# Two per-head factors spread over rows by transfers through DRAM instead of by products, with new figures for transfers in the planner

## The chip, the cores and the metric

The kernel runs on one core of one Trainium2 chip. Its engines are TensorE (PE, with its weight loads shown apart as PEld), VectorE (DVE), ScalarE (ACT), GpSimd (POOL) and SyncE (SP), which issues all transfers here. The metric is device microseconds of one execution; the time given is the median of three runs.

## What is computed

One step of a hybrid trunk layer: 2048 prompt tokens and 8 sample sequences of 16 tokens, width 1024. After an RMS norm one projection feeds three head groups: forgetting attention (6 heads), RWKV-7 time mixing (6 heads of 64) and cross-attention to 256 memory tokens (4 heads). Each group is gated, and an output projection with the residual ends the layer. The change touches the RWKV group. Cut to it, the reference is:

```
kk = k * ph(k_k)
kk = kk * lax.rsqrt(jnp.maximum(jnp.sum(kk * kk, axis=-1, keepdims=True), 1e-24))
...
S, y = rwkv_scan(s0, r, decay, k, v, kk, a)     # S <- S diag(w) + S (-kk)^T (a*kk) + v^T k
mu = jnp.mean(y, axis=-1, keepdims=True)
var = jnp.mean(jnp.square(y - mu), axis=-1, keepdims=True)
yn = (y - mu) * lax.rsqrt(var + GN_EPS) * ph(gn_w) + ph(gn_b)
```

Both the key's norm and the group norm's variance are one number for each token and head, with which all 64 rows of that head are multiplied.

## The kernel before, in words

The RWKV group holds its data with a pair of heads on the 128 partitions (64 rows a head) and tokens along the free dimension. The first phase of the program runs over four blocks of 512 tokens, and in each over three head pairs p; the 128 sample tokens come as three more groups, one behind each of three prompt groups. So there are 15 groups: 12 of 512 tokens (nt = 4 tiles of 128) and 3 of 128 (nt = 1). For a block, the normalised input xk is projected with weights that are split in two parts (tiles w, read back from the DRAM copy w_d from the second block on): pjd for the columns that stay transposed, pjt for q, k, v of the attention. A group passes through rwkv_in, rwkv_mid, rwkv_scan and rwkv_out, and projections of other columns lie between them.

per_head (line 342) sums the squares of a head's 64 rows by products with a matrix of ones (PSUM tile pss) and copies the result, a 128 x 2nt tile with tokens on partitions, to inv. In rwkv_in it is the key's norm: DVE takes the maximum and the reciprocal (lines 379 and 380), and since kk enters the update twice, that reciprocal is applied once: it is spread and multiplied into AR's first half (line 400), which the Gram products gr read with bk. In rwkv_out it is the variance: DVE and POOL make the inverse root (rsqrt_small, line 68 for DVE, 62 for POOL), and the spread factor is multiplied into ysb, half of tile yd (line 649).

spread (line 353) turns such a tile into 128 rows x 128nt tokens: for each token tile and head one product of the column, broadcast to 64 columns, with the identity. That is 8 calls of mm for 512 tokens and 2 for 128, into the single PSUM buffer "ra" that pss, zw, za and pbn use as well. The tile yd shares its buffer "bt" with rwkv_mid's tile bt. In the profile nearly every matmul has line 59 (mm), and DVE and POOL operations have 62, 65 and 68 (tt, stt, ts): they are told apart by their tiles.

The second phase is the attention, the sample sequences' attention and the output projection; it reuses the first phase's memory. There too a factor is spread over rows through DRAM (rc to rd, then two transfers rb<-rd, lines 1190 and 1193).

The order on every engine is not that of the code. _arrange collects all instructions, gives each a cost (_Op), and _schedule places them one by one, each where its engine could start it earliest, in a simulated run; it tries several rankings, keeps the shortest and writes that order out. An SP transfer has an issue time (own), a time on the wire (wire, one after another for all transfers) and a time to land (time). SP's queue works in order: an instruction there that waits holds up all behind it. A change of any cost can move instructions anywhere in the program.

Of the kernel before, what the change touches and what calls it, by code (L numbers as in the profile page):

```python
# [9 lines left out]
F32 = mybir.dt.float32  # L10
# [41 lines left out]
def kernel(ctx: ExitStack, tc: tile.TileContext, I: dict, O: dict):  # L52
    nc = tc.nc
    V, S, G, PE, SY = nc.vector, nc.scalar, nc.gpsimd, nc.tensor, nc.sync
# [3 lines left out]
    def mm(out, lhsT, rhs, start=True, stop=True):  # L58
        PE.matmul(out, lhsT, rhs, start=start, stop=stop, skip_group_check=True)  # L59

    def tt(e, out, a, b, op):
        e.tensor_tensor(out=out, in0=a, in1=b, op=op)  # L62

    def stt(out, a, s, b, op0, op1):
        V.scalar_tensor_tensor(out=out, in0=a, scalar=s, in1=b, op0=op0, op1=op1)
# [9 lines left out]
    M, A_, SUB, MAX = ALU.mult, ALU.add, ALU.subtract, ALU.max  # L75
# [21 lines left out]
    ident = ct("ident", [128, 128])  # L97
# [25 lines left out]
    with ExitStack() as p1:  # L123
# [12 lines left out]
        vh = c1t("vh", [128, 24])  # L136
# [25 lines left out]
        sm = pools(p1, "sm", bufs=2)  # L162
# [175 lines left out]
        def at(h, a=0):  # L338

            return slice(64 * (h ^ a), 64 * (h ^ a) + 64)  # L340

        def per_head(sq, nt):

            pss = ps.tile([128, 512], F32, tag="ra", name="pss")
            for t in range(nt):
                for j in range(2):
                    mm(pss[64 * j:64 * j + 64, 2 * t:2 * t + 2], sq[:, 128 * t + 64 * j:128 * t + 64 * j + 64],
                       bones[:, 0:128:64].bitcast(F32))
            r = sm.tile([128, 8], F32, tag="inv", name="inv")[:, :2 * nt]
            V.tensor_copy(r, pss[:, :2 * nt])  # L350
            return r

        def spread(r, nt, pool, tag):

            out = pool.tile([128, 512], F32, tag=tag, name="spr")
            for t in range(nt):
                for h in range(2):
                    mm(out[at(h), 128 * t:128 * t + 128], r[:, 2 * t + h:2 * t + h + 1].to_broadcast([128, 64]), ident)
            return out[:, :128 * nt]

        def rwkv_in(p, k, r, v, g, sample, tok0):

# [34 lines left out]
            V.tensor_copy(wc, wx[:, :, seg])  # L397

            stt(seg3(ar[:, 0, :n]), seg3(k), col(NKK), wx[:, :, 0:seg], M, M)
            tt(V, ar[:, 0, :n], ar[:, 0, :n], spread(inv, nt, ps, "ra"), M)  # L400
            tt(V, seg3(ar[:, 1, :n]), seg3(r), wx[:, :, 1:seg + 1], M)

            ts(G, e5, e3, col(HKA), col(OHKA), M, A_)
# [233 lines left out]
        def rwkv_out(p, sample, n, nch, tok0, gt, bv, py, so):  # L637

            nt = n // 128
            two = rv.tile([128, 2, 512], F32, tag="bt", name="yd")  # L640
            ysb, sq = two[:, 0, :n], two[:, 1, :n]
            S.copy(ysb, py.rearrange("p c t -> p (c t)")[:, :n])
            yc = pg.tile([128, 512], F32, tag="gr", bufs=2, name="yc")[:, :n]
            mm(yc, centre, ysb)
            S.activation(sq, yc, AF.Square)
            S.copy(ysb, yc)
            r = per_head(sq, nt)
            rsqrt_small(r, r, 2 * nt, 1.0 / 64, GN_EPS)
            stt(ysb, ysb, vh[:, GW5 + p:GW5 + p + 1], spread(r, nt, ps, "ra"), M, M)
            stt(bv, bv, vh[:, GB5 + p:GB5 + p + 1], ysb, A_, A_)  # L650
            tt(V, bv, bv, gt, M)
            SY.dma_start(o_d[384 + 128 * p:384 + 128 * (p + 1), tok0:tok0 + n], bv)
            if sample:
                for c in range(2):
                    pt = pg.tile([128, 512], F32, tag="gr", bufs=2, name="pst")
                    for s in range(4):
                        PE.transpose(pt[0:64, 128 * s:128 * s + 128], so[:, c, s, :], ident)
                    sst = rv.tile([64, 4, 2, 64], F32, tag="gm", name="sst", bufs=2)
                    S.copy(sst, pt[0:64, :].rearrange("p (s h k) -> p s h k", h=2, k=64))
                    for h in range(2):  # L660
                        SY.dma_start(O["rs_s"][4 * c:4 * c + 4, 2 * p + h].rearrange("s v k -> v s k"), sst[:, :, h, :])
# [882 lines left out]
class _Op:  # L1544


    def __init__(self, i, eng):
        ins, outs = ([s.bass_ap for s in x if getattr(s, "bass_ap", None) is not None] for x in (i.ins, i.outs))
        aps, kind = ins + outs, type(i).__name__
        space = lambda a: str(getattr(a.tensor, "_space", ""))  # L1550
        sizes = [_free(list(a.ap)) for a in ins]
        n = max(_free(list(a.ap)) for a in aps)
        self.shares = self.reads = self.two = False
        if eng == "PE":
            x, w = ins[:2]
            wide = str(i.ins[0].dtype) == "dt.float32"
            rows, cols, self.n = list(x.ap)[0][1], sizes[1], sizes[0]
            self.turns, self.plain, self.bf = i.is_transpose, wide and not i.is_transpose, "bf" in str(i.ins[0].dtype)
            size = lambda k: 32 if k <= 32 else 64 if k <= 64 else 128
            self.shape = (size(rows), size(cols)) if self.plain else (128, 128)  # L1560
            self.place = tuple(i.tile_position or (0, 0))
            self.load = 2 * cols / 2.4
            self.cells = self.n * rows / 128 * ((2 if self.turns else 4) if wide else 1)
            if self.plain:
                self.own = 2 * max(cols, self.n) / 1.2 + (10 if rows > 64 else 2)
                self.time = self.own + 165
            else:
                self.own = 30 if self.turns else 40 if self.bf else max(3 + 0.4453 * self.n, 12 + 0.4219 * self.n)
                self.time = 275 if self.turns else self.n / 2.4 + 170
            return  # L1570
        psum = any("PSUM" in space(a) for a in aps)
        scalar = n > 1 and any(k == 1 for k in sizes)
        if eng == "SP":
            size = 4 * list(outs[0].ap)[0][1] * _free(list(outs[0].ap))
            run = min(4 * list(a.ap)[-1][1] if list(a.ap)[-1][0] == 1 else 4 for a in aps)
            self.own, self.wire = (430 if run < 512 else 360), size / 230
            self.time = 1300 + (size / 140 - size / 230) * (run < 1024) / 2
            return
        wide = sum(k > 1 and "SB" in space(a) for k, a in zip(sizes, ins))
        self.reads = wide > 0  # L1580
        if eng == "Activation":
            t = (140 if psum else 178) + 0.833 * n + 90 * scalar
        elif eng == "Pool":
            if "pow" in str(getattr(i, "op", "")):
                t = 360 + 163 * n
            elif "Memset" in kind:
                t = 95 + 0.83 * n
            elif "ScalarPtr" in kind:
                t = 210 + 1.09 * n if n > 256 else 190 + 2.1 * n
            else:  # L1590
                t = 200 + 2.13 * n
        else:
            self.two = not psum and sum(k > 1 for k in sizes) == 1 and ("TensorCopy" in kind or "TensorScalar" in kind)
            self.shares = self.two or wide > 1
            if "Memset" in kind:
                t = max(65, 57 + 1.04 * n)
            elif "Reciprocal" in kind:
                t = 148 + 6.3 * n
            elif "Custom" in kind:
                t = 220 + 1.042 * n  # L1600
            else:
                t = 155 + 0.521 * n if self.two else 152 + 1.042 * n + 52 * (scalar and "ScalarPtr" in kind)
        self.time, self.own = t, t - _BACK[eng]
# [178 lines left out]
def _schedule(p, rank, stay, loose=()):  # L1782
# [33 lines left out]
    while len(order) < count:  # L1816
# [37 lines left out]
        c = cost[nodes[x][0]]  # L1854
        if e == "SP":
            free[e] = s + c.own
            wire = max(wire, s + c.own + 300) + c.wire
            end[x] = wire + c.time
        elif e == "PE":
            for j, k in enumerate(nodes[x]):  # L1860
                t, till = array.run(cost[k], r)
                s, end[x] = (t if not j else s), max(end[x], till)
            free[e] = array.last
        else:
            wait = 0
            if e == "DVE" and c.shares:
                wait = max([b - s for a, b, z in held["Pool"][-4:] if a < s < b and (c.two or z.reads)], default=0)
            elif e == "Pool":
                wait = max([b - s for a, b, z in held["DVE"][-4:] if a < s < b and (z.two or c.reads)], default=0)
            free[e], end[x] = s + wait + c.own, s + wait + c.time  # L1870
            if e == "Pool" or c.shares and e == "DVE":
                held[e].append((s + wait, free[e], c))
# [156 lines left out]
```

## Time and profile before

| | |
|---|---|
| runs (median, lowest, highest) | 1825.83, 1825.49, 1829.49 us |
| profiled execution: time / span | 1826.43 / 1824.6 us |
| mean granted TensorE clock | 0.967 |
| DMA queue's share of 16 engines | 48.5% |
| HBM read / written | 202.58 / 87.08 MB |
| first phase ends, attention begins | about 1131 us |

The page's busy shares are averages over the whole span, so the stages have to be looked at one by one. In rows of groups, "out<-in" names the tiles (buffer numbers left out), then come partitions x elements, the count, busy us, mean ns of one and the idle time of the engine just before them. In timelines the first two columns are start and length in us, and brackets give the idle time before a row and what ended it. "SPq" rows are issues of transfers by SP; their length is SP's issue time, not the time until the data lands.

### The profile page before, as it was taken

How to read it: one execution, taken by the hardware profiler on the slowest of the kernel's cores; microseconds unless marked ns; L12 is line 12 of the kernel's file. 1: busy time of each engine (PE TensorE's matmuls, PEld its weight loads, DVE VectorE, ACT ScalarE, POOL GpSimd, SP SyncE). 2: the span in 40 equal slices, each digit the busy share in tenths (PEclk: the TensorE clock that was granted, in tenths of full speed). 3: DMA queues.
4: the chain of work that ended last, by engine and by line, in shares of the span. 5: the costliest groups of instructions: out<-in, count | busy, mean ns of one | idle time of the engine just before them, and what ended most of it. 6: DMA issues, size and time to landing. Idle time of an engine off the chain costs nothing.

```text
span 1824.6 us, 41978 instructions
## 1 busy us (share of the span) xinstructions
PE 1756.1 (96%) x16883; PEld 1395.2 (76%) x16883; DVE 927.2 (51%) x2102; ACT 895.5 (49%) x1755; POOL 793.7 (43%) x818
## 2 busy tenths in 40 slices
PE   7999999999999999998999998999999999999998
PEld 6998999788877888876788886666666566667776
DVE  5544444464445553545743453767455545575213
ACT  5424343524234323324332434887888477986452
POOL 4555342242131341311332152567676265876452
PEclk8999999999999999999999999899999589999999
DMA  6767463745446464535363353434437542354422
GB/s 193 242 206 242 138 203 113 240 164 174 139 153 203 148 220 163 161 102 178 108 220 131 124 156 120 155 117 156 152 124 242 181 160 87 124 174 145 159 99 97
DMA packets 208905, 292.42 MB, mean 160 GB/s; under 512 B 56844, under 2 KB 161790, under 8 KB 192838
## 3 DMA queue, kind: packets, MB, share of 16 engines
q1 hardware_dynamic: 208710, 289.73, 48.5%
q8 instruction: 133, 2.18, 0.5%
q14 instruction: 62, 0.51, 0.1%
HBM read 202.58 MB, written 87.08 MB: 159 GB/s over the span
## 4 chain that ended last, share of the span: by engine, by line
PE 79%; DVE 7%; ACT 5%; DMA 3%; issue 3%; SPq 1%; POOL 1%; DVEq 0%; ACTq 0%; POOLq 0%
PE pjd L59 20%; PE pjt L59 12%; PE py L59 10%; PE po L59 9%; PE pS L59 7%; PE pm L59 4%; PE sc L59 2%; PE sy L59 1%; PE gr L59 1%; PE pz L59 1%; PE pa L59 1%; PE spr L59 1%; DMA w<-w_d 1%; PE gw L59 1%; PE gx L59 1%
## 5 line engine op out<-in xcount | busy, mean ns | idle before, releaser
L59 PE MATMUL pjd<-xk,w 128*128 128x512 f32 (+4 forms) x2280 | 522.6, 373 | 8.9 <-DVE xk L62 4.1
L59 PEld LDWEIGHTS pjd<-xk,w 128*128 128x128 f32 (+1 forms) x2280 | 380.4, 190 | 75.6 <-issue 10.2
L62 POOL TENSOR_TENSOR Pl<-P,Ph 128x512 fp32r<-128x512 f32 (+3 forms) x272 | 315.4, 1170 | 158.5 <-ACT Ph L1137 122.2
L59 PE MATMUL pjt<-w,xk 128*128 128x256 f32 x2040 | 282.4, 290 | 6.8 <-issue 3.5
L59 PEld LDWEIGHTS pjt<-w,xk 128*128 128x128 f32 x2040 | 260.1, 193 | 16.0 <-issue 7.8
L59 PE MATMUL py<-W,oh 128*128 128x512 f32 x816 | 248.7, 404 | 1.4 <-DVE rb L1179 1.4
L1134 ACT ACTIVATE P<-pS,NB 128x512 f32<-128x512 f32 x240 | 148.7, 623 | 70.8 <-PE pS L59 48.6
L59 PEld LDWEIGHTS py<-W,oh 128*128 128x128 f32 x816 | 150.1, 189 | 40.3 <-DVE rb L1179 1.8
L1078 DVE TENSOR_REDUCE mx<-pm 128x1 f32<-128x512 f32 (+2 forms) x240 | 140.8, 605 | 63.5 <-PE pm L59 60.7
L59 PE MATMUL pS<-Q,K 128*128 128x512 f32 (+1 forms) x480 | 162.6, 397 | 7.8 <-ACT P L1134 3.2
L1137 ACT CAST Ph<-P 128x512 fp32r<-128x512 f32 (+3 forms) x272 | 151.8, 564 | 18.6 <-PE po L59 13.7
L59 PE MATMUL po<-Ph,vt 128*65 128x512 f32 x480 | 156.8, 380 | 0.9 <-ACT ob L1157 0.5
L62 DVE TENSOR_TENSOR xo<-py,xo 128x512 f32<-128x512 f32 x68 | 46.7, 687 | 154.6 <-PE py L59 154.6
L59 PEld LDWEIGHTS pS<-Q,K 128*128 128x128 f32 (+1 forms) x480 | 88.7, 197 | 40.2 <-ACT P L1134 14.0
L62 POOL TENSOR_TENSOR nr<-nr,mhalf 128x8 f32<-128x8 f32 (+2 forms) x43 | 60.9, 1416 | 115.5 <-DVE nr L68 102.0
L59 PE MATMUL pm<-K,Q 67*128 67x512 f32 (+2 forms) x240 | 97.8, 424 | 2.8 <-DVE mx L1078 2.1
L62 POOL TENSOR_TENSOR w<-wraw,w 128x1024 fp32r<-128x1024 f32 (+1 forms) x34 | 79.8, 2348 | 43.8 <-ACT w L197 43.4
L59 PE MATMUL po<-Pl,vt 128*65 128x512 f32 x240 | 90.5, 377 | 0.2
L59 PEld LDWEIGHTS po<-Ph,vt 128*65 128x65 f32 x480 | 64.5, 142 | 26.5 <-issue 3.0
L710 ACT COPY qk<-pjt 128x512 f32<-128x512 f32 (+1 forms) x47 | 26.2, 565 | 102.5 <-PE pjt L59 63.3
L62 POOL TENSOR_TENSOR oh<-ot,oh 128x384 fp32r<-128x384 f32 (+2 forms) x38 | 45.9, 1207 | 61.6 <-ACT oh L1340 51.0
L59 PEld LDWEIGHTS pm<-K,Q 67*128 67x128 f32 x240 | 49.4, 209 | 20.3 <-DVE mx L1078 8.3
(399 smaller groups left out, 2847.4 us busy)
## 6 DMA issues: line engine op xcount, KB each, us to landing
w<-w_d SPq DMA_DIRECT2D x84, 1024.0 KB
w_d<-w SPq DMA_DIRECT2D x28, 1024.0 KB
y_d<-xo SPq DMA_DIRECT2D x21, 512.0 KB
wraw<-in_w_in SPq DMA_DIRECT2D x36, 256.0 KB
xo<-in_x SPq DMA_DIRECT2D x17, 512.0 KB
xo<-y_d SPq DMA_DIRECT2D x17, 512.0 KB
xt<-in_x SPq DMA_DIRECT2D x24, 256.0 KB
xraw<-in_xT SPq DMA_DIRECT2D x24, 256.0 KB
```

The lines of the kernel that those rows point to most:

```text
L59: PE.matmul(out, lhsT, rhs, start=start, stop=stop, skip_group_check=True)
L62: e.tensor_tensor(out=out, in0=a, in1=b, op=op)
L710: S.copy(o_, out)
L1078: V.tensor_reduce(out=q["mx"][:, h, t, c0 // 512:c0 // 512 + 1], in_=pm[:, :n], op=MAX, axis=AX.X)
L1134: S.activation(P_[:, c0:], pS[:, c0:], AF.Exp, bias=NB[:, qb, 2 * hp + h, kt:kt + 1] if fox else 0.0)
L1137: S.copy(Ph[:, c0:], P_[:, c0:])
```

## The change

spread no longer multiplies. It transposes the 128 x 2nt tile r to 2nt rows of 128 tokens (PE, PSUM tile spt), copies that to SBUF (ACT, tile spr), writes it to DRAM (SP, sp_d, 4 KB), and reads it back for each head with one transfer that gives the same 128nt numbers to 64 partitions (128 KB each). per_head now places its columns head by head, so that a head's rows lie together in sp_d. The target is given by the caller: AR's second half, which holds the squares before and the receptance after, and sq, the other half of yd. The products that follow read SBUF in place of PSUM. Besides, the planner's figures for transfers change.

```
                 for j in range(2):
-                    mm(pss[64 * j:64 * j + 64, 2 * t:2 * t + 2], sq[:, 128 * t + 64 * j:128 * t + 64 * j + 64],
+                    mm(pss[64 * j:64 * j + 64, t:t + nt + 1:nt], sq[:, 128 * t + 64 * j:128 * t + 64 * j + 64],
                        bones[:, 0:128:64].bitcast(F32))
...
-        def spread(r, nt, pool, tag):
-
-            out = pool.tile([128, 512], F32, tag=tag, name="spr")
-            for t in range(nt):
-                for h in range(2):
-                    mm(out[at(h), 128 * t:128 * t + 128], r[:, 2 * t + h:2 * t + h + 1].to_broadcast([128, 64]), ident)
-            return out[:, :128 * nt]
+        def spread(out, r, nt):
+
+            n = 2 * nt
+            pt = ps.tile([128, 512], F32, tag="ra", name="spt")
+            PE.transpose(pt[0:n, 0:128], r, ident)
+            rr = sm.tile([8, 128], F32, tag="spr", name="spr", bufs=1)[:n]
+            S.copy(rr, pt[0:n, 0:128])
+            sp_d = dt("sp_d", [8, 128], bufs=4)
+            SY.dma_start(sp_d[:n], rr)
+            for h in range(2):
+                SY.dma_start(out[at(h)], sp_d[nt * h:nt * h + nt].rearrange("t p -> (t p)").partition_broadcast(64))
...
-            tt(V, ar[:, 0, :n], ar[:, 0, :n], spread(inv, nt, ps, "ra"), M)
+            spread(ar[:, 1, :n], inv, nt)
+            tt(V, ar[:, 0, :n], ar[:, 0, :n], ar[:, 1, :n], M)
...
-            stt(ysb, ysb, vh[:, GW5 + p:GW5 + p + 1], spread(r, nt, ps, "ra"), M, M)
+            spread(sq, r, nt)
+            stt(ysb, ysb, vh[:, GW5 + p:GW5 + p + 1], sq, M, M)
...
-            self.own, self.wire = (430 if run < 512 else 360), size / 230
-            self.time = 1300 + (size / 140 - size / 230) * (run < 1024) / 2
+            self.own, self.wire = (430 if run < 512 else 360), size / (270 if run < 1024 else 340)
+            self.time = 700
...
-            wire = max(wire, s + c.own + 300) + c.wire
+            wire = max(wire, s + c.own + 600) + c.wire
```

PE around the first inverse norm, before (AR_0_117 is AR's first buffer; zw and za are products of the decay and the learning rate):

```order
L59 MATMUL pss<-bones,AR_0_117 64x2 x8
L59 MATMUL pjd<-xk,w 128x256 x3
L59 MATMUL zw<-LW,WUP 128x512
L59 MATMUL pjd<-xk,w 128x256 x12
L59 MATMUL za<-LW,WUP 128x512
L59 MATMUL pjd<-xk,w 128x256 x9
L59 MATMUL pjd<-xk,w 128x384 x2
L59 MATMUL spr<-ident,inv 64x128 x8
L59 MATMUL pjd<-xk,w 128x384 x22
L59 MATMUL pjt<-w,xk 128x256 x15
L59 MATMUL gr_795<-AR_0_117,bk 64x128
```

The same place on PE after the change:

```order
L59 MATMUL pss<-bones,AR_0_117 64x2 x8
L59 MATMUL pjd<-xk,w 128x256 x12
L59 MATMUL pjd<-xk,w 128x384
L59 MATMUL pjd<-xk,w 128x256
L59 MATMUL pjd<-xk,w 128x384 x6
L59 MATMUL zw<-LW,WUP 128x512
...
L357 MATMUL spt<-ident,inv 8x128
L59 MATMUL pjd<-xk,w 128x256 x23
L59 MATMUL pjd<-xk,w 128x384 x24
L59 MATMUL pjt<-w,xk 128x256 x58
L59 MATMUL gr_794<-AR_0_117,bk 64x128
```

Between the spread and the first Gram product stood 37 projection matmuls, and there stand 105 now.

SP at the same place, after the change (wraw and w_d are weights read and their split copy written):

```order
L196 DMA wraw<-in_w_in 128x4x128 x2
L200 DMA w_d<-w 128x2048
L361 DMA sp_d<-spr 8x128
L363 DMA AR_0_117<-sp_d 64x512 x2
L196 DMA wraw<-in_w_in 128x4x256
L200 DMA w_d<-w 128x2048
```

The broadcasts follow straight on the write that they wait for, and weights come behind them. So it is in 14 of the 30 spreads; in the other 16 one to nine other transfers stand between.

PE at the end of the first phase, before (the last group norm; pst turns the RWKV state for the output, pt and pS are the attention's first products):

```order
L59 MATMUL pss<-bones,yd 64x2 x8
L59 MATMUL pjd<-xk,w 128x512 x9
L59 MATMUL spr<-ident,inv 64x128 x8
L927 MATMUL pst<-ident,ST 64x128 x3
L998 MATMUL pt<-ident,tok 128x128 x8
```

And after the change:

```order
L59 MATMUL pss<-bones,yd 64x2 x8
L59 MATMUL sc<-st,AD 128x64
L59 MATMUL pjd<-xk,w 128x512 x9
L357 MATMUL spt<-ident,inv 8x128
L59 MATMUL pjd<-xk,w 128x512 x9
L754 MATMUL ptok<-ident,tsb 128x128 x4
L933 MATMUL pst<-ident,ST 64x128 x3
L1004 MATMUL pt<-ident,tok 128x128 x8
```

Nine projection matmuls and four transposes stand now between the last spread's step on PE and the attention's first products, where only pst stood.

## The prediction

> **What bounds the kernel now.** I read first the page's busy times and its chain, then busy time by stage, then the added and removed tiles, and last single moments in the timelines. The page says which engine is full and which work the end hangs on:
>
> ```profile
> PE 1756.1 (96%) x16883; PEld 1395.2 (76%) x16883; DVE 927.2 (51%) x2102; ACT 895.5 (49%) x1755; POOL 793.7 (43%) x818
> PE 79%; DVE 7%; ACT 5%; DMA 3%; issue 3%; SPq 1%; POOL 1%; DVEq 0%; ACTq 0%; POOLq 0%
> ```
>
> TensorE is busy for 1756.1 of 1824.6 us and carries 79% of the chain that ends last; DMA carries 3%. The other engines are at half. By stage (columns: stage, length, busy time of PE, PEld, DVE, ACT and POOL with instruction counts, granted clock, DMA share, GB/s), where the first two rows are the projections and the RWKV groups, and the rest is attention and output:
>
> ```profile
> 0.00:50.00 50.00, 39.62 (x181) 34.61 (x182) 29.85 (x69) 29.03 (x65) 23.05 (x34) 0.90 0.70 210
> 50.00:1135.00 1085.00, 1051.62 (x13148) 901.06 (x13147) 538.04 (x1388) 388.69 (x812) 357.13 (x391) 0.99 0.51 167
> 1135.00:1400.00 265.00, 258.62 (x1216) 176.09 (x1214) 157.70 (x271) 217.13 (x396) 175.37 (x165) 0.96 0.47 150
> 1400.00:1475.00 75.00, 69.50 (x384) 44.39 (x382) 43.62 (x100) 39.16 (x77) 27.14 (x32) 0.66 0.60 199
> 1475.00:1825.00 350.00, 336.70 (x1964) 239.03 (x1962) 157.97 (x279) 221.44 (x408) 210.98 (x198) 0.98 0.38 131
> ```
>
> Both spreads lie in the stage 50 to 1135 us: PE is idle there for only 33.4 of 1085 us, at a granted clock of 0.99. So there a microsecond of TensorE work is nearly a microsecond of time, as long as other matmuls can move into its place. The DMA engines are half free (0.51).
>
> **What is removed.** The spread's products, from the matmul groups with shapes kept apart (busy us, mean ns, idle before), and one of them in PE's timeline, between two projections:
>
> ```profile
> L59 PE MATMUL spr<-ident,inv 128*64 128x128 f32 x408 | 28.9, 280 | 0.0
> ...
> 214.13 0.28 PE L59 MATMUL pjt<-w,xk 128*128 128x256 f32 x1
> 214.34 1.09 PE L59 MATMUL spr<-ident,inv 128*64 128x128 f32 x16
> 215.36 0.44 PE L59 MATMUL pjd<-xk,w 128*128 128x384 f32 x1
> ```
>
> 408 records are 204 calls of mm (two passes each): 12 full spreads of 8 calls at each of two places, and 3 sample spreads of 2 calls at each. A full one holds PE from 214.34 to 215.36, 1.02 us; 24 of them are 24.5, and the group with the six small ones is 28.9. No idle stands before it, so PE reached each with its operand ready. Removed: **-28.9 us** of a full engine.
>
> **What PE does instead.** One transpose per spread, of a 128x8 tile against the identity. The nearest row is the transpose of a 128x9 tile; for a lower bound, four wide transposes back to back:
>
> ```profile
> L853 PE MATMUL psh<-ident,sho 128*9 128x128 f32 x13 | 3.3, 272 | 0.0
> ...
> 1131.35 0.63 PE L998 MATMUL pt<-ident,tok 128*128 128x128 f32 x4
> ```
>
> 3.3 / 13 = 0.25 us each; back to back it is (0.63 - 0.27) / 3 = 0.12, with 0.27 as the length of a lone one (272 ns). The new ones stand alone between matmuls of other shapes, so I take the first: 30 x 0.25 = **+7.6 us**, with 3.6 and 8.2 (30 x 0.272) as ends. The Trainium skill (TensorEngine Tiling, Key Properties) says that a change of tiling mode drains the engine; by it the transpose, a narrow tile among full ones, would cost its lone 0.27 and the sum would stand 0.6 us higher. The 128x9 rows, at 0.25, nearly agree.
>
> **What goes to other engines, and what hides it.** ACT gets 30 copies like the first row below (237 ns), 7 us on an engine that is busy for 388.7 of 1085 us. DVE's two products read SBUF in place of PSUM. Their times now (min/median/max ns) are the second and third row; with all operands in SBUF the like is the fourth:
>
> ```profile
> L855 ACT COPY shr<-psh 9x128 f32<-9x128 f32 x1 | 0.2, 237 | 0.0
> ...
> L62 DVE TENSOR_TENSOR AR<-AR,spr x15: 273/674/687, 74.9 to 1020.4; 128x512 f32<-128x512 f32 x12, 128x128 f32<-128x128 f32 x3
> L65 DVE SCALAR_TENSOR_TENSOR yd<-yd,vh,spr x15: 348/746/748, 215.5 to 1130.2; 128x512 f32<-128x512 f32 x12, 128x128 f32<-128x128 f32 x3
> ...
> L62 DVE TENSOR_TENSOR ob<-ob,rb x19: 680/694/1668, 1185.4 to 1722.0; 128x512 f32<-128x512 f32 x19
> ```
>
> The median stays, and now and then one may take 1 us more; DVE is half idle in that stage, so all this is 0. The 90 new transfers carry 24 x 260 KB and little else: at 167 GB/s in a stage with DMA half idle, no bound.
>
> What costs is latency. A spread now is a 4 KB write, whose landing SP awaits, and two broadcasts of 128 KB. Near rows: 64 KB and 8 KB landing, from the chain; and the same pair of broadcasts of the attention stage, from SP's first issue to the release of DVE, behind a 512 KB store:
>
> ```profile
> 303.83 1.94 DMA ld<-yt
> ...
> 309.04 1.65 DMA xd<-ld
> ...
> 1717.69 1.25 SPq L1193 DMA_DIRECT2D rb<-rd  x2
> 1721.99 0.69 DVE L62 TENSOR_TENSOR ob<-ob,rb 128x512 f32<-128x512 f32 x1 [4.72 <-DMA rb<-rd]
> ```
>
> 1.65 + (1721.99 - 1717.69) = 5.95 us, and with transpose and copy (0.5) a round trip of 6.5 us in place of 1.1. The Trainium skill (DMA: Bandwidth & Descriptors, Anatomy of one DMA) gives a transfer a fixed cost of about 2.0 us, mostly the wait for the write's receipt, and its Rules for kernel authors count transfers under 64 KB as mostly overhead; both speak against the change. By 2.0 for the write the round trip would be 6.9 us, and the tail below and the sum 0.4 us later. The 8 KB row, 1.65, is less.
>
> Cover for it: the inverse norm (DVE's reciprocal) is ready long before the Gram products gr that use it, or shortly before. The rows come in pairs, ready and used; the first and third pair are the first head pair of a token block, the second is the usual case, the fourth the group norm's product and the next writer of its buffer:
>
> ```profile
> 68.86 0.20 DVE L380 RECIPROCAL inv<-inv 128x8 f32<-128x8 f32 x1
> 77.25 0.43 PE L59 MATMUL gr<-AR,bk 64*64 64x128 f32 x2
> ...
> 141.20 0.19 DVE L380 RECIPROCAL inv<-inv 128x8 f32<-128x8 f32 x1
> 194.31 1.10 PE L59 MATMUL gr<-AR,bk 64*64 64x128 f32 x32
> ...
> 359.73 0.20 DVE L380 RECIPROCAL inv<-inv 128x8 f32<-128x8 f32 x1
> 369.43 1.10 PE L59 MATMUL gr<-AR,bk 64*64 64x128 f32 x32
> ...
> 351.86 0.75 DVE L65 SCALAR_TENSOR_TENSOR yd<-yd,vh,spr 128x512 f32<-128x512 f32 x1 [4.42 <-PE spr L59]
> 353.49 0.42 ACT L548 COPY bt<-pbt 128x128 f32<-128x128 f32 x2
> ```
>
> Usually there are 53 us (141.20 to 194.31). The first head pair of a block has 8.4 to 9.7 us, against a round trip plus product of 7.2: covered, and in the new order 105 projection matmuls stand between the first transpose and gr, where 37 did. The group norm's factor holds the yd buffer some 5 us longer; only a sample group's bt (353.49, right behind the last reader of yd) follows closely, and PE has projections meanwhile. So 0 here, with the rival below for where it fails.
>
> **The end of the stage** has no such cover. The last group norm's chain ends in DVE's product, and POOL fills the attention's K right behind it:
>
> ```profile
> 1129.28 4.71 DMA vtok<-v_d
> ...
> 1130.20 0.74 DVE L65 SCALAR_TENSOR_TENSOR yd<-yd,vh,spr 128x512 f32<-128x512 f32 x1
> 1130.96 0.99 POOL L990 MEMSET K<- 1x512 f32 x2
> ```
>
> If K waits for yd's memory, it comes 5 us later; but vtok lands only at 1134.0 (1129.28 + 4.71), so 3 of the 5 are covered: **+2 us**, ends 0 and 5.
>
> **The planner's new figures** change the whole order, in attention too. For 8 KB they go from 2.08 us (430 + 300 + 36 + 1300 + 11 ns) to 1.76, where the row has 1.65; for 64 KB from 2.25 to 1.85 (row 1.94); for a 1 MB weight load from 6.5 to 4.74, where the trace has
>
> ```profile
> 392.96 5.98 DMA w<-w_d
> ```
>
> So they are nearer for small transfers, and 1.2 us too hopeful for big ones, where the old were 0.5 too cautious. Too hopeful a load makes PE wait; too cautious a one only has other work put first. I take 0, and as ends a third of the 33.4 us of idle either way, an estimate: -11 to +11.
>
> **Sum**, against the profiled execution's 1826.43 us (span 1824.6 and 1.8 around it; the median of the three timed runs, 1825.83, is the same within 0.03%): -28.9 + 7.6 + 2 + 0 = -19.3, so **1807.1 us**. The ends of transposes, tail and planner give 1826.4 - 28.9 + 3.6 + 0 - 11 = 1790 and 1826.4 - 28.9 + 8.2 + 5 + 11 = 1822.
>
> **Rivals.** *SP holds the spreads up (slower).* SP is one queue in order, and it stands for matmuls in front of weight loads (total us, times, longest):
>
> ```profile
> SPq L192 <- PE pjd L59: 104.7, 45, 7.9
> ...
> 825.00:850.00 25.00, 19.96 (x398) 14.38 (x396) 9.22 (x14) 9.78 (x20) 5.19 (x6) 0.86 0.67 235
> ```
>
> A write or a broadcast behind such a load is late by up to 7.9 us, and in 14 of the 30 spreads the broadcasts follow straight on the write, so that SP itself stands for its landing, with weights queued behind. The tight places are four (first head pairs) and three (sample groups). A hold of 7.9 less the spare 1.2 to 2.5 us (8.4 or 9.7 less 7.2) leaves PE some 6 us idle, and the clock drops with it (0.86 where PE was busy for 19.96 of 25 us). It decides from a mean of 2.8 us at the seven places (19.3 / 7); 6 us at four of them, 24 us, give 1807 + 24 = 1831. Against it: the planner knows of SP's order, and PE is idle for little now despite those waits. *A longer cold stretch (no change).* The stage 1400 to 1475 had a clock of 0.66, so some 51 us (0.34 / 0.5 of 75) at half clock, worth up to 25 us. It is planned anew: 36 us more of it cost 18, which gives 1825. *A shorter one (faster still)*: half of it gone is -12, which gives 1795. *That the change does less than it says*: not so, the new order has no spr product and 30 transposes.
>
> **Chances.** Forecast (1800 to 1818) 0.58; part of the gain eaten, but still faster, 0.04; faster still 0.14; no change 0.12; slower 0.12. A difference of 0.2%, 3.7 us, is about what a measurement of this kernel can tell from none. Faster 0.58 + 0.04 + 0.14 = 0.76, same 0.12, slower 0.12. The range runs from 1793 (most of the faster case) to 1826 (all the forecast's ends and half of no change), leaving out some 0.2.
>
> **What would show it.** Right: PE's busy time falls by about 21 us, all of it before the attention, whose start moves from 1135 to about 1117; PE's idle stays near 70 us; gr waits for bk and not for AR's broadcast; the psh-like transposes take 0.25. Wrong: PE waits on transfers sp_d or on AR; SP's waits for the sp_d landing grow past 60 us with PE's waits on weights; the clock by stage differs from 0.99 before or 0.66 in the sample stage; or the attention stage, untouched by the spread, changes its length by more than 5 us.

## The result, and the profile after

| | before | after |
|---|---|---|
| median of 20 runs each, on one chip | 1828.22 us | 1813.53 us |
| lowest to highest | 1820.38 to 1837.51 us | 1805.14 to 1831.94 us |
| ratio, with its 95% interval | 1 | 0.9927 (0.9909 to 0.9946) |
| profiled execution: time / span | 1826.43 / 1824.6 us | 1817.21 / 1815.4 us |

The change makes the kernel 0.7% faster, 14.7 us; the forecast was 19.3 us. The size is near, but the time did not come from where the forecast looked for it. First the busy times on after's page, and its chain:

```profile
PE 1728.0 (95%) x16505; PEld 1376.4 (76%) x16505; DVE 942.7 (52%) x2102; ACT 902.1 (50%) x1785; POOL 800.1 (44%) x818
...
PE 62%; DMA 12%; DVE 7%; ACT 6%; SPq 3%; issue 3%; POOL 2%; DVEq 0%; ACTq 0%; POOLq 0%
```

PE is busy for 28.1 us less, yet the span is only 9.2 us shorter: idle time rose from 68.5 to 87.4 us, and DMA's share of the chain from 3% to 12%. Busy time by stage in after, with the same edges as before except the last (the columns are as in the prediction):

```profile
0.00:50.00 50.00, 36.82 (x151) 31.24 (x152) 25.75 (x55) 26.67 (x59) 21.59 (x30) 0.90 0.66 192
50.00:1135.00 1085.00, 1038.17 (x12790) 888.79 (x12789) 549.76 (x1388) 391.93 (x836) 358.63 (x377) 0.98 0.52 172
1135.00:1400.00 265.00, 256.31 (x1177) 175.69 (x1176) 157.83 (x276) 213.84 (x393) 174.43 (x175) 0.92 0.46 147
1400.00:1475.00 75.00, 70.03 (x491) 47.41 (x489) 58.88 (x120) 57.17 (x113) 42.62 (x50) 0.98 0.75 251
1475.00:1816.00 341.00, 326.63 (x1905) 233.22 (x1903) 150.51 (x265) 212.47 (x387) 202.88 (x188) 0.98 0.39 131
```

In the second stage PE is idle for 46.8 us where it was 33.4, and the attention still begins where it did. In the fourth the clock is 0.98 where it was 0.66: 491 matmuls fit where 384 did.

To add this up I cut each profiled execution at pst, the end of the first phase (1131.0 us before, 1135.1 after), took windows of 10 us, and split each in three: PE's busy time times its granted clock (work, in us at full clock), busy time times the rest (lost to the clock), and idle time. The sums in us:

| first phase | length | work | lost to clock | idle |
|---|---|---|---|---|
| before | 1131.2 | 1075.1 | 15.1 | 41.0 |
| after | 1135.3 | 1050.6 | 24.6 | 60.0 |
| **second phase** | | | | |
| before | 693.4 | 630.4 | 35.4 | 27.6 |
| after | 680.1 | 626.8 | 25.8 | 27.4 |

The first phase, where the spread stands, has 24.5 us less work and is 4.1 us longer. The second, which the spread does not touch, is 13.3 us shorter.

The new transposes on PE and their copies on ACT in after (min/median/max ns), and who waits for the broadcasts:

```profile
L357 PE MATMUL spt<-ident,inv x30: 270/272/415, 73.5 to 1132.5; 128*8 128x128 f32 x24, 128*2 128x128 f32 x6
L359 ACT COPY spr<-spt x30: 237/255/257, 74.2 to 1132.8; 8x128 f32<-8x128 f32 x24, 2x128 f32<-2x128 f32 x6
...
DVE AR L62: 18.2, 9
DVE yd L65: 10.8, 10
```

A transpose lasts 272 ns, the forecast's upper end; what it costs PE is less and is worked out further down. DVE waits for the broadcasts at 19 of the 30 spreads. What SP and PE wait for in the first phase of after (total us, times, longest):

```profile
SPq L361 <- ACT spr L359: 77.5, 21, 16.3
SPq L363 <- DMA sp_d<-spr: 46.0, 24, 6.4
SPq L461 <- DMA ld<-yt: 22.6, 11, 6.0
...
PE gw L59 <- DVE x L474: 13.6, 10, 3.6
PE yc L59 <- ACT yd L647: 5.1, 2, 3.4
PE pjd L59 <- DMA w<-w_d: 3.0, 4, 1.0
```

PE hardly stands for weights. SP stands 77.5 us more for ACT's copies, in front of the spread's writes; the forecast had counted only the landing, 46.0 us. PE's greatest wait is new: gw, the first product with a triangular inverse, which needs x, DVE's transpose of xd. That inverse, too, goes through DRAM and back, in four dependent steps (gm to ld, ld to yt, yt to ld, ld to xd). Its groups on DVE show what x itself waits for. Before:

```profile
DMA xd<-ld: 1.3, 2
```

After:

```profile
DMA xd<-ld: 44.0, 12
```

Twelve groups of 512 tokens, and DVE stands at every one, 3.7 us each. One place in after's chain of waits shows how a spread and an inverse meet (start, length; gaps under 0.1 us are left out):

```profile
209.03 0.12 PE spt L357
209.18 0.26 ACT spr L359
209.46 4.36 DMA sp_d<-spr
213.87 0.46 SPq L363
214.38 3.03 DMA yd<-sp_d
217.51 0.75 DVE yd L65
218.26 0.08 DVE ytmp L62
218.34 0.71 DVE bv L65
219.04 0.10 DVE yt L62
219.16 1.94 DMA ld<-yt
...
224.31 1.96 DMA xd<-ld
226.29 0.46 DVE x L474
226.79 0.75 PE gw L59 x50
```

The round trip takes 8.5 us here, from 209.03 to 217.51. DVE waits for its end with the group norm's product, and behind that in its queue stand the last two steps (ytmp, yt) of another group's inverse, whose transfers follow one after another until gw. So the hold-up was real at this place, but on DVE's queue and by way of a different chain than the forecast's.

### The profile page after: what moved, and what is told of

Read it like the earlier page. It is cut to its first block, busy times and chain, and to the rows that moved or that the text cites. A ratio compares the mean times of both kernels' runs of the same rounds, so it can differ in the third digit from the quotient of the medians.

```text
span 1815.4 us, 41404 instructions
## 1 busy us (share of the span) xinstructions
PE 1728.0 (95%) x16505; PEld 1376.4 (76%) x16505; DVE 942.7 (52%) x2102; ACT 902.1 (50%) x1785; POOL 800.1 (44%) x818
## 4 chain that ended last, share of the span: by engine, by line
PE 62%; DMA 12%; DVE 7%; ACT 6%; SPq 3%; issue 3%; POOL 2%; DVEq 0%; ACTq 0%; POOLq 0%
PE pjd L59 13%; PE py L59 9%; PE po L59 9%; PE pjt L59 8%; PE pS L59 6%; PE pm L59 4%; SPq L461 2%; PE sc L59 2%; DMA ld<-yt 2%; DMA w<-w_d 1%; DMA mg_d<-gth 1%; DMA yd<-sp_d 1%; DMA xd<-ld 1%; PE sy L59 1%; PE gw L59 1%
## 5 line engine op out<-in xcount | busy, mean ns | idle before, releaser
L59 PE MATMUL pjd<-xk,w 128*128 128x512 f32 (+5 forms) x2280 | 546.1, 380 | 18.3 <-DVE xk L62 4.8
L59 PEld LDWEIGHTS pjd<-xk,w 128*128 128x128 f32 (+1 forms) x2280 | 385.5, 192 | 84.8 <-issue 7.5
L59 PE MATMUL pjt<-w,xk 128*128 128x256 f32 x2040 | 295.0, 290 | 0.9 <-issue 0.9
L59 PEld LDWEIGHTS pjt<-w,xk 128*128 128x128 f32 x2040 | 268.3, 192 | 12.0 <-issue 5.2
L59 PE MATMUL pS<-Q,K 128*128 128x512 f32 (+2 forms) x480 | 164.0, 396 | 4.2 <-ACT P L1140 2.5
L59 PEld LDWEIGHTS pm<-K,Q 67*128 67x128 f32 x240 | 48.7, 204 | 24.5 <-DVE mx L1084 9.0
```

## The experiments

The change has two halves, the spread and the planner's figures. e1 to e4 take them apart; e5 to e8 turn one figure of after and of before by 3%; e9 to e11 look at the spread's transfers, and e12 is e1 with a figure turned. e1 to e4 ran on one chip and e5 to e12 on another, each beside before, and both sets of figures occur on both. Every one of them is planned anew, so that its order differs from before's and after's everywhere. The sums by phase, made as above from each kernel's profiled execution ("old" is 230 bytes a ns with 1300 and 300 ns, "new" is 270/340 with 700 and 600):

| kernel | spread | figures | ratio to before | first: work | first: lost + idle | second: work | second: lost + idle | x waits for xd |
|---|---|---|---|---|---|---|---|---|
| before | products | old | 1 | 1075.1 | 56.1 | 630.4 | 63.0 | 1.3 |
| e7 | products | old, 223 | 1.0072 | 1075.0 | 70.4 | 629.6 | 60.5 | 16.7 |
| e8 | products | old, 237 | 0.9927 | 1077.5 | 50.3 | 628.8 | 59.9 | 10.7 |
| e4 | none | old | 1.0086 | 1047.4 | 105.3 | 621.9 | 65.5 | 16.2 |
| e1 | transfers | old | 1.0360 | 1047.4 | 154.9 | 628.8 | 67.7 | 23.0 |
| e12 | transfers | old, 237 | 1.0025 | 1052.8 | 89.7 | 628.4 | 60.6 | 9.0 |
| e2 | products | new | 0.9971 | 1080.8 | 67.3 | 630.3 | 43.7 | 23.2 |
| e3 | none | new | 0.9766 | 1047.4 | 62.0 | 629.3 | 45.6 | 33.0 |
| after | transfers | new | 0.9927 | 1050.6 | 84.6 | 626.8 | 53.2 | 44.0 |
| e5 | transfers | new, 262/330 | 0.9904 | 1051.5 | 71.7 | 627.7 | 47.8 | 37.4 |
| e6 | transfers | new, 278/350 | 0.9964 | 1056.9 | 86.0 | 628.9 | 50.9 | 29.7 |
| e9 | transpose and copy only | new | 0.9945 | 1053.0 | 79.9 | 628.0 | 49.2 | 29.8 |
| e10 | transfers that nobody reads | new | 0.9891 | 1048.6 | 78.7 | 625.0 | 53.0 | 25.2 |
| e11 | transfers on ACT's queue | new | 1.0115 | 1047.9 | 126.2 | 628.0 | 44.6 | 27.7 |

A profiled execution is one of several and can lie off its kernel's median (e5's by 0.7%, 1800.47 against 1813.24 us), so single entries are good to some us only: the second phase's work, where all kernels run the same products, goes from 621.9 to 630.4. What holds over several rows is used.

**e1, the spread with the old figures.**

```
-            self.own, self.wire = (430 if run < 512 else 360), size / (270 if run < 1024 else 340)
-            self.time = 700
+            self.own, self.wire = (430 if run < 512 else 360), size / 230
+            self.time = 1300 + (size / 140 - size / 230) * (run < 1024) / 2
...
-            wire = max(wire, s + c.own + 600) + c.wire
+            wire = max(wire, s + c.own + 300) + c.wire
```

> The new spread with the planner's old figures. Theory H (hold-up): the spread's transfers stand in SP's queue ahead of the inverse's transfers ld and xd, PE waits for the inverse (gw), and this, not the figures, eats the 21 us of matmuls; so the first phase still ends near 1131 to 1136 us, the second stays at some 693, ratio 0.998 to 1.005. Rival F (figures too hopeful): the waits come from a plan that counts transfers too short; with the old figures the first phase ends near 1112, ratio about 0.99. Rival O (order): any replanning moves each phase by some 10 us, and neither number will be met.

Measured: 1894.56 us, 1.036 (1.0332 to 1.0388). All three theories put it near or below 1. The busy time of the worst stretch, some 100 us before the phase's end, and the matmuls that end PE's wait there:

```profile
1075.00:1100.00 25.00, 7.08 (x257) 6.24 (x258) 7.32 (x23) 7.13 (x16) 5.70 (x6) 0.56 0.33 105
...
1088.83 1.07 PE L59 MATMUL gw<-x,gm 32*32 32x32 f32 x64 [14.64 <-DVE x L474]
```

PE is busy for 7.08 of 25 us, and no other engine for more than 7.32. PE stands 14.64 us for x, at the end of an inverse's chain; projections were still to come (96 pjd and 96 pjt start after 1110 us), but this order has none between 1074 and 1110. So what shows here is an order that leaves one chain uncovered; why the planner made it was not found.

**e2, the new figures without the spread.** The edit is the reverse of e1's, on the kernel before.

> The old spread by products, with the planner's new figures. H: the first phase ends near 1131 as before and the second takes some 680, as in the changed kernel, so ratio about 0.993. F: the first phase grows by the waits of a too hopeful plan, to some 1150, the second takes 680, ratio 1.003. O: anything between 0.99 and 1.01.

Measured: 1824.08 us, 0.9971 (0.9947 to 0.9994). Its phases, 1148 and 674 us, come nearest to theory F's. In the first it has 11.2 us more of idle and clock than before, in the second 19.3 less. The second difference is borne out by the other rows (14.4 us in the mean); the first lies within what before itself moves by in e7 and e8 (50.3 to 70.4).

**e3, no spread at all.** The factors are not applied; AR's product becomes one of the same length with a zero in it, so that AR's first half is zero.

```
-            spread(ar[:, 1, :n], inv, nt)
-            tt(V, ar[:, 0, :n], ar[:, 0, :n], ar[:, 1, :n], M)
+            stt(ar[:, 0, :n], ar[:, 0, :n], 0.0, ar[:, 1, :n], M, M)
...
-            spread(sq, r, nt)
             stt(ysb, ysb, vh[:, GW5 + p:GW5 + p + 1], sq, M, M)
```

> New figures, and the spreading left out altogether: no products, no transposes, no transfers; the two factors are computed and not applied (AR's first half becomes zero by a product of the same length on DVE). H: the first phase loses all 28.9 us of matmuls and has no new waits, so it ends near 1102, and with 680 for the second the ratio is about 0.976. F: the hopeful plan keeps its waits, first phase near 1118, ratio 0.985. O: 0.97 to 0.99.

Measured: 1786.05 us, 0.9766 (0.9738 to 0.9795). That is theory H's number. Against e2, with the same figures, it is 38 us for 29 us of products.

**e4, the same with the old figures** (e3 with e1's edit).

> As the run before (spreading left out, AR's first half zero), with the old figures. H and F alike: first phase near 1102, second some 693, ratio 0.983; if this does not show, PE is not what the first phase hangs on. O: 0.97 to 0.995.

Measured: 1846.63 us, 1.0086 (1.0062 to 1.0109). No theory had this: the same 29 us of products taken out of before make it 17 us slower. Work falls in the table as it should (1075.1 to 1047.4); idle and clock take it back and more.

**e5 and e6, after with one figure turned by 3%.**

```
-            self.own, self.wire = (430 if run < 512 else 360), size / (270 if run < 1024 else 340)
+            self.own, self.wire = (430 if run < 512 else 360), size / (262 if run < 1024 else 330)
```

and 278 and 350 in e6.

> The changed kernel with the wire's figures set 3% lower (262 and 330 bytes a ns): the same instructions, another order. Theory O (order): at so small a change every phase is redrawn, so the time moves by 10 us or more, and the ratio to the kernel before lies anywhere from 0.985 to 1.01; only the spread of several such orders says what the change is worth. Rival S (steady): the new figures describe the chip better and give good orders throughout, ratio 0.990 to 0.996, first phase within 5 us of 1135, second within 5 us of 680.

> The changed kernel with the wire's figures 3% higher (278 and 350). O: as the run before, 0.985 to 1.01, and not the same as it. S: 0.990 to 0.996.

Measured: e5 1813.24 us, 0.9904 (0.9876 to 0.9932); e6 1822.05 us, 0.9964 (0.9944 to 0.9985). Both ratios lie in theory O's range, and in or just beside S's, but e5's first phase ends at 1123 and e6's at 1143, outside theory S's 5 us around 1135.

**e7 and e8, before with one figure turned by 3%.**

```
-            self.own, self.wire = (430 if run < 512 else 360), size / 230
-            self.time = 1300 + (size / 140 - size / 230) * (run < 1024) / 2
+            self.own, self.wire = (430 if run < 512 else 360), size / 223
+            self.time = 1300 + (size / 140 - size / 223) * (run < 1024) / 2
```

and 237 in e8.

> The kernel before with its one wire figure 3% lower (223 for 230): the same instructions. The runs so far had three old-figure programs, at 1829, 1847 (with 29 us of matmuls fewer) and 1895 us. O: the order of the kernel before was a lucky one among those of the old figures, so this is slower, ratio 1.01 to 1.03. S: the old figures give steady orders for this program, ratio 0.997 to 1.004, and it was the transfers in SP's queue that cost in the spread-only run.

> The kernel before with the wire figure 3% higher (237 for 230). O: ratio 1.01 to 1.03, and not the same as the run before. S: 0.997 to 1.004.

Measured: e7 1841.8 us, 1.0072 (1.0041 to 1.0104); e8 1817.0 us, 0.9927 (0.9902 to 0.9953). Both theories missed: before's order was neither a lucky one nor a steady one. With the very same instructions before moves by 0.7% either way, as much as the whole change. So one order against one order does not tell what the change is worth. The means of three are 1.0000 for before, e7 and e8, and 0.9932 for after, e5 and e6, but e8's 0.9927 is after's own ratio: that any order by the change beats any by the old kernel is not shown. Nor is a gain of the spread alone: e2, with the new figures and the products, has 0.9971.

**e9, transposes and copies, but no transfers.** The factors are not applied.

```
-            sp_d = dt("sp_d", [8, 128], bufs=4)
-            SY.dma_start(sp_d[:n], rr)
-            for h in range(2):
-                SY.dma_start(out[at(h)], sp_d[nt * h:nt * h + nt].rearrange("t p -> (t p)").partition_broadcast(64))
...
-            tt(V, ar[:, 0, :n], ar[:, 0, :n], ar[:, 1, :n], M)
+            stt(ar[:, 0, :n], ar[:, 0, :n], 0.0, ar[:, 1, :n], M, M)
```

> The changed kernel with the transposes and their copies, but without the three transfers; the factors are not applied (AR's first half becomes zero, as in the left-out runs). Between spreading left out (0.9766) and the changed kernel with its two neighbours in order (mean 0.9929) lie 30 us; the prediction had 9.6 for that. Theory Q (queue): the transfers hold up SP's order; rival L (latency): the factor comes late; both say that without transfers the ratio is 0.9766 + 7.6/1829 = 0.981. Rival T (transposes dear): 0.988 to 0.993. O (order): each run is only good to some 0.004.

Measured: 1819.01 us, 0.9945 (0.9924 to 0.9966), far from the 0.981 of Q and L and nearest to T.

**e10, all transfers, but into a scratch tensor in DRAM that nobody reads.**

```
-            spread(ar[:, 1, :n], inv, nt)
-            tt(V, ar[:, 0, :n], ar[:, 0, :n], ar[:, 1, :n], M)
+            spread(dt("dead", [128, 512], bufs=4)[:, :n], inv, nt)
+            stt(ar[:, 0, :n], ar[:, 0, :n], 0.0, ar[:, 1, :n], M, M)
...
-            spread(sq, r, nt)
+            spread(dt("dead", [128, 512], bufs=4)[:, :n], r, nt)
```

> The changed kernel with all its transfers, but with the broadcasts going to a scratch tensor in DRAM that nobody reads; the factors are not applied. SP issues and waits as in the changed kernel, and no product waits for a broadcast. Q: nothing is won, 0.990 to 0.994. L: the wait is gone, 0.981 to 0.984. T: as the run before, near 0.990 in both.

Measured: 1806.16 us, 0.9891 (0.986 to 0.9922), nearest to Q and T. In e9 nothing can wait for the transfers, since there are none, and in e10 nothing waits for the broadcasts; yet idle and clock of the first phase, 79.9 and 78.7 us, lie among those of after, e5 and e6 (71.7 to 86.0). So the first phase loses about as much without the round trip. These are two single orders, and orders of one program differ by 14 us: a share of some us is not excluded, but the round trip is not the main cause.

**e11, the three transfers on ACT's queue.**

```
-            SY.dma_start(sp_d[:n], rr)
+            S.dma_start(sp_d[:n], rr)
             for h in range(2):
-                SY.dma_start(out[at(h)], sp_d[nt * h:nt * h + nt].rearrange("t p -> (t p)").partition_broadcast(64))
+                S.dma_start(out[at(h)], sp_d[nt * h:nt * h + nt].rearrange("t p -> (t p)").partition_broadcast(64))
...
+        if "DMA" in kind and eng == "Activation":
+            self.own, self.time = 60, (1700 if "DRAM" in space(outs[0]) or n <= 128 else 2600)
+            return
```

> The changed kernel with the spread's three transfers issued by ACT in place of SP (the planner counts them there with 60 ns of issue and 1.7 and 2.6 us to land). Q: SP is free of them, PE's waits for the inverse (gw) fall, ratio 0.983 to 0.988. L: the factor comes as late as before or later, 0.991 to 0.996; and ACT, which now waits for sp_d's landing in its own order, delays its copies out of PSUM, which would make it slower than that.

Measured: 1846.74 us, 1.0115 (1.008 to 1.015). SP's queue is free of the spread here, and the kernel is slower. In its PE waits the wait that the forecast named is the second largest:

```profile
PE gr L59 <- DVE AR L62: 11.3, 3, 5.6
```

PE waits for the scaled AR three times, 11.3 us in all; in after it does so once, for 0.6. The expectation's reason, that ACT's copies stand behind the wait for the landing, fits this but was not measured by itself.

**e12, e1 with 237 in place of 230.**

> The spread by transfers with the planner's old figures, its wire figure at 237 for 230 (the kernel before gained 0.7% from the same). O: the 65 us lost by the spread-only run were one unlucky order, with its stall at the end of the first phase; ratio 0.99 to 1.015. Rival P (planner): the old figures do not fit the spread's transfers in any order, ratio 1.02 to 1.04.

Measured: 1832.96 us, 1.0025 (1.0007 to 1.0044). The same 3% that made before 0.7% faster brings e1's 1.036 down to this. So theory O holds, and P does not. In neither of the two orders does the spread gain with the old figures.

**What the table shows, over all of it.** Two things hold in every row, and a third only in the mean.

Work follows the instructions. The mean of the first phase is 1077.1 us for the four kernels with products, 1047.4 for the two without a spread, 1051.1 for the eight with transposes. So the products cost 29.7 us at full clock. The transposes cost 3.7 in the mean, with single rows from 0 to 9.5.

The second phase goes with the figures. Lost and idle time there is 59.9 to 67.7 us in all six orders by the old figures and 43.7 to 53.2 in all eight by the new, 62.9 and 48.5 in the mean: 14.4 us, whatever the spread is. Nearly all of it is the clock: time lost to it is 34.4 us in the mean of the old orders and 21.0 of the new. The place is 200 to 400 us into that phase, around the start of the sample sequences' part: there the old orders lose 13.3 to 25.6 us to the clock and the new ones 1.7 to 10.0. In most old orders it is one stretch at about half, in e8 a milder one (0.64 to 0.72). Two kernels that differ in figures and not in the spread, at the same distance from their phase's start; e7:

```profile
1425.00:1475.00 50.00, 46.09 (x267) 29.27 (x267) 28.36 (x67) 21.73 (x43) 11.70 (x15) 0.57 0.58 187
```

and e2:

```profile
1428.00:1478.00 50.00, 48.39 (x385) 32.78 (x383) 40.40 (x91) 39.65 (x81) 32.46 (x38) 0.97 0.82 275
```

PE is nearly as busy in both, with 267 matmuls in one and 385 in the other. What in the old orders brings the clock down there was not found: PE's longest wait in the stretch is 1.4 us in e7 and 0.6 in e2.

The wait of x for xd is longer by the new figures, spread or no spread: 31.3 us in the mean of eight orders, against 12.8 of six. But the two sets touch (e1 has 23.0, e2 23.2), and the wait does not go with the time: e3 has 33.0 us of it and the least idle and clock of all new orders in the first phase, e6 has 29.7 and 24 us more. The figures give the wait a sign: the 8 KB pieces that end an inverse are planned to land 1.76 us after their issue, where the old figures said 2.08, and the 64 KB write before them after 1.85 instead of 2.25. In after's chain of waits the eleven last pieces of an inverse land after 1.60 to 3.10 us, with 1.74 in the middle, so that date is no worse than the old one. The seven writes ld<-yt there land after 1.94 to 6.61, all later than planned; the latest of them, and the piece that follows it:

```profile
481.03 6.61 DMA ld<-yt
...
492.07 1.68 DMA xd<-ld
```

So if a date was too early, it was the write's. But the chain shows the late transfers rather than all, the old date was too early for five of the seven as well, and 0.4 us of difference a group does not explain 23 to 44 us: that the figures cause the wait in this way is argued, not shown.

## Why the prediction was right, and where it was wrong

**The sum of PE's work was right.** -28.9 for the products measured -29.7; +7.6 for the transposes measured 3.7 by the mean of the sums of work, close to the forecast's lower end of 3.6. A single one lasts 272 ns, as in the quoted tile, but the next matmul does not wait for that (PE's timeline of after, in its last spread):

```profile
1132.49 0.27 PE L357 MATMUL spt<-ident,inv 128*8 128x128 f32 x1
1132.52 2.33 PE L59 MATMUL pjd<-xk,w 128*128 128x512 f32 x9
```

It starts 0.03 us later, so no drain shows here. The length of a row was the wrong price, and the back-to-back one was nearer.

**The step that failed: "So there a microsecond of TensorE work is nearly a microsecond of time, as long as other matmuls can move into its place."** By the means of three orders each, the first phase has 22.9 us less work and 21.8 us more of idle and clock (58.9 to 80.8), so 1.0 us of it arrives. The 33.4 us of idle time before said how well that one order was packed, not that a new order would be packed as well; e4 has 27.7 us less work in the first phase than before, and its first phase is 21.6 us longer. "PE idle stays near 70", and a start of the attention at 1117, were wrong: 87 and 1135. The forecast's own sign for this, PE's waits on sp_d or AR, showed in after only once, for 0.6 us. PE's largest new wait there, gw on x, is 13.6 of the 19.0 us by which idle time rose in the first phase; but e2 and e3, without the spread, have it too (8.9 and 7.5).

**"The planner's new figures ... I take 0" failed too.** Some 14 us were gained in the second phase. In the first, x's wait grew, but what that cost is not shown. Calling the new figures "nearer for small transfers" holds for the 8 KB pieces (1.74 against a planned 1.76) and not for the 64 KB write, which the quoted row, 1.94 us, showed at its shortest: after's chain has it at 1.94 to 6.61. The forecast's range of 11 us either way for this term was about the right width, and its rival of a shorter cold stretch in the sample stage was what happened: 0.66 became 0.98, though after also runs longer cold right behind the start of the attention.

So the forecast was near by luck, as a sum of two errors: by the means of three orders 20 us too much from the first phase (-21.3 forecast, -1.0 measured) and 14 too little from the second (+2 forecast, the tail, and -12.3 measured).

**The rival "SP holds the spreads up"** is not what decided: SP's waits for the landing of sp_d are 46.0 us, under the 60 named, PE waits only 3.0 us for weights, and e9, which has no transfers, is not faster than after. e10 speaks against the other half, a factor that comes late. e11 can't tell, since it moves the waits to ACT. A hold did occur, in DVE's queue (the chain at 209 us); its sum could not be told apart from the order's own scatter.

**The tail** of 2 us came out at 1.8: from pst to the first product with K it is 6.7 us before (1131.0 to 1137.73) and 8.5 after, in PE's timeline and the transfers there:

```profile
1133.08 0.30 SPq L361 DMA_DIRECT2D sp_d<-spr  x1
1136.43 0.46 SPq L363 DMA_DIRECT2D yd<-sp_d  x1
1137.56 0.45 SPq L363 DMA_DIRECT2D yd<-sp_d  x1
1139.72 0.52 POOL L996 MEMSET K<- 1x512 f32 x1
1142.19 0.75 DVE L65 SCALAR_TENSOR_TENSOR yd<-yd,vh 128x512 f32<-128x512 f32 x1 [0.74 <-DMA yd<-sp_d]
1143.62 0.44 PE L59 MATMUL pm<-K,Q 67*128 67x128 f32 x1 [1.82 <-DMA K<-nc_d]
```

The number is luck, for its mechanism was another: the first MEMSET of K, at 1139.72, does not wait for yd's product at 1142.19. PE waits for a transfer into K from nc_d, which SP issues after the broadcasts.

**What stays open.** The cause of the first phase's 21.8 us: which part belongs to the transposes (e9 has 17.9 us more of idle and clock than e3), which to the waits on x, and which to the luck of an order; three orders of the same program spread over 14 to 20 us there. Why the spread loses with the old figures in both orders, and what sets the clock back in the sample stage, were not settled. e3, e4, e9 and e10 compute on other numbers (AR's first half is zero), and that the clock does not depend on them was not tested; e4 lost 82.9 us to the clock even so, before 50.5. The fastest kernel that still computes all is e5, but its interval overlaps after's.

## What to carry to other kernels

When a planner sets the whole order, a sum of the work removed forecasts the work, not the time: plan both versions at two or three neighbouring values of one figure, and believe only a difference that is larger than their scatter. Split each phase into work at the granted clock, time lost to the clock, and idle time; here the first followed the edit to a few us, and the gain was decided by the other two. When a landing time is tuned in the plan, compare it with many landings of each size and kind, above all along a chain of dependent transfers, and not with one row.

## What was not expected of the hardware

The granted clock stood at one half (0.50) for tens of us in phases where PE was nearly always busy; after's own stretch at the start of the attention is one:

```profile
1150.00:1175.00 25.00, 23.77 (x80) 15.52 (x79) 22.76 (x41) 18.79 (x38) 10.05 (x12) 0.50 0.57 181
```

PE was busy for 23.77 of 25 us and did 80 matmuls. All time lost to the clock is 50.5 us in before and 50.4 in after; it only moved. And the same 4 KB write landed after 1.22 us at one spread of after and after 4.36 at another; the first of these rows:

```profile
469.56 1.22 DMA sp_d<-spr
470.84 0.45 SPq L363
471.34 3.88 DMA yd<-sp_d
475.35 0.75 DVE yd L65
```

From the transpose (469.14) to DVE's product the round trip took 6.2 us there and 8.5 at 209 us; the forecast's 6.5 was the short case.
